# A two-block transformer kernel on one core: another order for one gate's loads, a place of the weights' ring for exponentials, 64-row products in alternation, and a later spare chunk

## The chip, the cores and the metric

The kernel runs on one core of a Trainium2 chip. The metric is the device time of one execution in microseconds (us); lower is better. Engines are named as in the profile: PE (TensorE, its weight loads apart as PEld), DVE (VectorE), ACT (ScalarE), POOL (GpSimd) and SP (SyncE, which here issues nearly all of the transfers).

## The reference

Two blocks follow each other on one sequence of 256 rows with 1024 features, all in float32. The first block has two layers, each with a mixer and a feed-forward part, and modulates both by a vector c:

```python
for i in range(2):
    mods = split(silu(c) @ w_ada[i] + b_ada[i], 6)          # sh1, sc1, g1, sh2, sc2, g2
    u = x * (1 + sc1) + sh1
    y = gla_mixer(u, ...) if i == 0 else chunk_attention(u, ...)   # 16 heads of 64
    x = layer_norm(ALPHA * x + (1 + g1) * y, ...)
    u = x * (1 + sc2) + sh2
    y = square(relu(u @ w1)) @ w2                            # 1024 -> 4096 -> 1024
    x = layer_norm(ALPHA * x + (1 + g2) * y, ...)
```

Attention is a softmax over q k' plus a bias per head. The second block is a hybrid mixer (a causal pool, and an attention of 8 heads of 64 over the best 64 keys, which an indexer with 8 heads of 64 scores) and a gated convolution network; both have dense products before and behind them.

## The kernel before, in words

**Products.** Every float32 product of the dense layers is made as three matmuls in a faster format (helper `mm3`, lines 266 to 268): the weight is split into a rounded part `hi` and a rest `lo`, the activations into `uh`/`hh` and `ul`/`hl`, and hi·uh, lo·uh and hi·ul are added up in one PSUM bank. Small products (attention scores, transposes, states) stay in float32.

**Weights.** They come in 316 chunks of 128 x 1024 floats (512 KB). `fetch` (L238) loads a chunk into `raw`, a ring of four places; ACT copies `hi` (L257) and DVE subtracts for `lo` (L262, in two halves near the ends of phases). `hi` and `lo` are rings of NB = 8 places. Some chunks are "spare": they are split into the memory of tiles that have nothing else to hold at that time (`qk0`/`v0` or `qk1`/`v1`), so that they take no place in the rings. `room()` says whether the next chunk may be loaded, and `prefetch` loads as far ahead as it allows.

**Phases.** Six phases use the chunks in order: the first mixer (chunks 16 to 36), feed-forward 1 (37 to 100), attention (101 to 132), feed-forward 2 (133 to 196), hybrid mixer (197 to 249), convolution network (250 to 315). `ENDS` holds 37, 101, 133, 197, 250, 316. The rows of the sequence are two halves, h = 0 and h = 1. A generator for each half walks through the chunks; h = 0 runs up to eight chunks ahead at a phase's start and end. A line of the program that `yield`s lets the loop go on to the next step of the one or the other half, so the order of instructions on every engine is the order in which these generators and the prefetch are called, moved a little by priorities.

**Modulation.** The w_ada product is made without PE: `ada_gen` loads 512 KB pieces into the same ring `raw` (L296) and adds them up on DVE, gates in a tile `acc` (L298), the others by rows (L300); eight pieces make one of shift, scale and gate. A gate's `acc` then becomes rows through two float32 matmuls (`gate_rows`, L325). A list `marks` holds pairs (chunk, steps): at a chunk between two marks, as many steps have been made as the line between them says, where a step is a piece or, once for every eight pieces, what closes their sum. All the loads, of weights and pieces, biases and rows, go through SP's one queue in program order.

**Attention.** `att_phase` handles the heads in two groups, g = 0 and 1, of eight. For each it makes q, k and v from chunks; while the v product runs, `core_scores` makes scores (L754), one bank of four heads (h = 0, 128 keys) or two heads (h = 1, 256 keys) at a time, adds the bias (L817, DVE), takes the maximum (L758, DVE), the exponentials with their sums (L760, ACT, one instruction for each head), and transposes them (L373, PE) into `pts` (L769, ACT). A head has 64 dimensions, so its product uses 64 of the 128 rows: the even heads of a pair lie on rows 0 to 63, the odd ones on rows 64 to 127. A bank holds heads of one parity. The hybrid mixer calls `core_scores` too; its indexer (L908) and the states of the first mixer (L727) are products of 64 rows of the same kind. `pts` lie in the tile `gnorm` for h = 0, and in `z` and `acc` for h = 1.

Of the kernel before, what the change touches and what calls it, by code (L numbers as in the profile page):

```python
# [20 lines left out]
NB = 8  # L21
# [164 lines left out]
class K:  # L186
# [450 lines left out]
    def gla_core(self, h, lr, q, k, v, box):  # L637
# [57 lines left out]
        S2 = self.states(h, 0, er, v, dec)  # L695
# [9 lines left out]
        if h == 0:  # L705
            self.S = S2
            self.S = self.states(h, 1, er, v, dec)
# [10 lines left out]
    def states(self, h, c, er, v, dec):  # L718

        nc = self.nc  # L720
        out = []
        r = slice(c * 64, c * 64 + 64)
        for j in range(2):
            p = self.pc()
            for d2 in range(2):
                d = j * 2 + d2
                nc.tensor.matmul(p[:, d2 * 256:d2 * 256 + 256], er[r, d * 128:d * 128 + 128], v[r, d * 256:d * 256 + 256], start=True, stop=True)  # L727
            S = self.sb(512, "bias", 4)
            if self.S is None:
                nc.scalar.activation(S, p, AF.Copy)  # L730
            else:
                for d2 in range(2):
                    hs = slice(d2 * 256, d2 * 256 + 256)
                    nc.vector.scalar_tensor_tensor(S[:, hs], self.S[j][:, hs], dec[:, j * 2 + d2, c:c + 1], p[:, hs], op0=ALU.mult, op1=ALU.add)
            out.append(S)
        return out
# [5 lines left out]
    def core_scores(self, h, qT, kT, pts, sums, score):  # L742
# [5 lines left out]
        last = None  # L748

        for n, hs in enumerate(self.banks(nb)):  # L750
            p = self.bank()
            for i, hd in enumerate(hs):
                r0 = (hd % 2) * 64
                nc.tensor.matmul(p[:, i * N:i * N + N], qT[r0:r0 + 64, hd // 2, :], kT[r0:r0 + 64, hd // 2, :N], start=True, stop=True)  # L754
            s = score(hs[0], nb, p)
            sv = s.rearrange("p (a n) -> p a n", n=N)
            mx = self.sb(4, "mx", 4)
            nc.vector.tensor_reduce(mx[:, :nb], sv, axis=AX.X, op=ALU.max, negate=True)  # L758
            for i in range(nb):
                nc.scalar.activation(sv[:, i, :], sv[:, i, :], AF.Exp, bias=mx[:, i:i + 1], accum_out=sums[:, hs[i]:hs[i] + 1])  # L760
            if last is not None:
                self.core_turn(last, pts[n - 1])
            last = s
            yield
        self.core_turn(last, pts[n])
# [31 lines left out]
    def halves(self, *tags):  # L797
        return [t[:, j * 512:j * 512 + 512] for t in (self.sb(1024, *g) for g in tags) for j in range(2)]

    def att_phase(self, h, after):  # L800
# [3 lines left out]
        for g in range(2):  # L804
# [66 lines left out]
    def hyb_phase(self, h, after):  # L871
# [32 lines left out]
        for hs in self.banks(nb):  # L904
            p = self.bank()
            for i, hd in enumerate(hs):
                r0 = (hd % 2) * 64
                nc.tensor.matmul(p[:, i * N:i * N + N], iqT[r0:r0 + 64, hd // 2, :], self.ikT[r0:r0 + 64, :N], start=True, stop=True)  # L908
            rl = self.cs()[:, :512]
            nc.scalar.activation(rl, p, AF.Relu, scale=0.125)  # L910
            for i, hd in enumerate(hs):
                if hd == 0:
                    nc.vector.tensor_scalar(sc, rl[:, 0:N], iw[:, 0:1], None, op0=ALU.mult)
                else:
# [478 lines left out]
```

## Time and profile before

| | |
|---|---|
| median of 3 runs | 1059.1 us (1054.99 to 1060.17) |
| the profiled execution | 1057.73 us, of which its span is 1055.9 us |
| granted TensorE clock, mean | 0.995 |
| PE busy | 1017.6 us, 96% of the span |
| DVE busy | 763.3 us, 72% |
| ACT busy | 567.6 us, 54% |
| transfers | 229 MB, 217 GB/s over the span |

The page is one execution. The shares are means over the whole span, and PE, the busiest, has about 38 us in which it is not busy; the places of these gaps can be read from the chain of waits and the timelines. A record's time on PE overlaps that of the next, so the cost of a matmul is seen in the distance between starts.

### The profile page before, as it was taken

How to read it: one execution, taken by the hardware profiler on the slowest of the kernel's cores; microseconds unless marked ns; L12 is line 12 of the kernel's file. 1: busy time of each engine (PE TensorE's matmuls, PEld its weight loads, DVE VectorE, ACT ScalarE, POOL GpSimd, SP SyncE). 2: the span in 40 equal slices, each digit the busy share in tenths (PEclk: the TensorE clock that was granted, in tenths of full speed). 3: DMA queues.
4: the chain of work that ended last, by engine and by line, in shares of the span. 5: the costliest groups of instructions: out<-in, count | busy, mean ns of one | idle time of the engine just before them, and what ended most of it. 6: DMA issues, size and time to landing. Idle time of an engine off the chain costs nothing.

```text
span 1055.9 us, 15168 instructions
## 1 busy us (share of the span) xinstructions
PE 1017.6 (96%) x5628; PEld 850.0 (80%) x5628; DVE 763.3 (72%) x1186; ACT 567.6 (54%) x869; POOL 33.8 (3%) x77
## 2 busy tenths in 40 slices
PE   6999999999998999999999999999999999999997
PEld 4777777898986758677889988777878788999996
DVE  6878898777677886749656644898445678877764
ACT  4664466545455454536655553576454378555543
POOL 0000200000000000000000000000000001000000
PEclk9999999999999999999999999999999999999999
DMA  9888868888885787825877654344346455655521
GB/s 341 331 298 301 309 201 282 306 304 298 284 297 179 218 295 247 286 92 184 287 229 249 227 166 145 120 145 149 106 164 213 162 179 182 217 185 192 183 80 40
DMA packets 69478, 228.98 MB, mean 217 GB/s; under 512 B 7430, under 2 KB 12806, under 8 KB 69404
## 3 DMA queue, kind: packets, MB, share of 16 engines
q1 hardware_dynamic: 69404, 228.01, 64.2%
q8 instruction: 44, 0.72, 0.3%
q14 instruction: 30, 0.25, 0.1%
HBM read 226.93 MB, written 1.05 MB: 216 GB/s over the span
## 4 chain that ended last, share of the span: by engine, by line
PE 63%; DVE 9%; DMA 7%; ACT 3%; issue 3%; POOL 1%; POOLq 0%; DVEq 0%; ACTq 0%; SPq 0%
PE ps L268 12%; PE ps L266 12%; PE ps L267 12%; PE y L266 8%; PE y L268 8%; PE y L267 7%; DMA raw<-in_w_dram 6%; DVE lo L262 2%; PE y L780 1%; PE pc L373 1%; ACT hi L257 1%; DMA raw<-in_ada_dram 1%; PE y L373 1%; PE y L754 1%; DVE x L393 1%
## 5 line engine op out<-in xcount | busy, mean ns | idle before, releaser
L262 DVE TENSOR_TENSOR lo<-raw,hi 128x1024 fp32r<-128x1024 f32 (+3 forms) x290 | 306.5, 1068 | 132.8 <-ACT hi L257 129.4
L257 ACT ACTIVATE hi<-raw 128x1024 fp32r<-128x1024 f32 (+2 forms) x250 | 262.4, 1054 | 252.1 <-PE y L268 66.9
L266 PE MATMUL ps<-hi,uh 128*128 128x512 f32 (+3 forms) x408 | 160.4, 394 | 2.3 <-ACT uh L365 0.9
L267 PE MATMUL ps<-lo,uh 128*128 128x512 f32 (+3 forms) x408 | 158.2, 388 | 1.2 <-DVE lo L1260 1.1
L266 PE MATMUL y<-hi,hh 128*128 128x512 f32 x378 | 152.9, 404 | 5.3 <-ACT hh L274 5.2
L268 PE MATMUL ps<-hi,ul 128*128 128x512 f32 (+3 forms) x408 | 157.5, 386 | 0.2 <-DVE ul L366 0.2
L267 PE MATMUL ps<-ul,hi 128*128 128x256 f32 x536 | 151.4, 282 | 0.0
L268 PE MATMUL ps<-uh,lo 128*128 128x256 f32 x536 | 151.1, 282 | 0.0
L266 PE MATMUL ps<-uh,hi 128*128 128x256 f32 x536 | 151.0, 282 | 0.0
L268 PE MATMUL y<-hi,hl 128*128 128x512 f32 x378 | 149.8, 398 | 0.4 <-DVE hl L275 0.4
L267 PE MATMUL y<-lo,hh 128*128 128x512 f32 x378 | 150.2, 397 | 0.0
L266 PEld LDWEIGHTS ps<-uh,hi 128*128 128x128 f32 x536 | 100.9, 188 | 2.3
L267 PEld LDWEIGHTS ps<-ul,hi 128*128 128x128 f32 x536 | 100.6, 188 | 2.3
L268 PEld LDWEIGHTS ps<-uh,lo 128*128 128x128 f32 x536 | 101.3, 189 | 0.0
L266 PEld LDWEIGHTS ps<-hi,uh 128*128 128x128 f32 x408 | 77.5, 190 | 19.3 <-ACT uh L365 1.5
L267 PEld LDWEIGHTS ps<-lo,uh 128*128 128x128 f32 x408 | 77.5, 190 | 16.8 <-DVE lo L1260 3.0
L268 PEld LDWEIGHTS ps<-hi,ul 128*128 128x128 f32 x408 | 77.4, 190 | 15.8 <-issue 0.9
L266 PEld LDWEIGHTS y<-hi,hh 128*128 128x128 f32 x378 | 71.5, 189 | 21.4 <-ACT hh L274 6.6
L268 PEld LDWEIGHTS y<-hi,hl 128*128 128x128 f32 x378 | 71.3, 189 | 18.2 <-DVE hl L275 1.2
L267 PEld LDWEIGHTS y<-lo,hh 128*128 128x128 f32 x378 | 71.4, 189 | 14.8 <-issue 0.7
L262 DVE TENSOR_TENSOR v<-raw,qk 128x1024 fp32r<-128x1024 f32 (+1 forms) x49 | 52.0, 1069 | 26.7 <-ACT qk L257 26.1
L257 ACT ACTIVATE qk<-raw 128x1024 fp32r<-128x1024 f32 x42 | 44.5, 1060 | 49.7 <-DMA raw<-in_w_dram 28.7
(290 smaller groups left out, 1500.0 us busy)
## 6 DMA issues: line engine op xcount, KB each, us to landing
raw<-in_w_dram SPq DMA_DIRECT2D x302, 512.0 KB, 4.3
raw<-in_ada_dram SPq DMA_DIRECT2D x80, 512.0 KB, 4.6
br<-in_rows_dram SPq DMA_DIRECT2D x12, 256.0 KB, 5.4
bias<-in_relb_dram SPq DMA_DIRECT2D x12, 256.0 KB, 6.2
lng<-in_rows_dram SPq DMA_DIRECT2D x5, 512.0 KB, 4.8
raw<-in_w_dram SPq DMA_DIRECT2D x8, 256.0 KB, 6.7
lnb<-in_rows_dram SPq DMA_DIRECT2D x4, 512.0 KB, 6.1
z<-in_ada_dram SPq DMA_DIRECT2D x3, 512.0 KB, 7.4
```

What stands on the lines that cost most here:

```text
L257: self.nc.scalar.activation(hi, raw, AF.Copy)
L262: self.nc.vector.tensor_sub(lo[:, sl], raw[:, sl], hi[:, sl].bitcast(F32))
L266: mm(out, xh, wh, start=start, stop=False)
L267: mm(out, xh, wl, start=False, stop=False)
L268: mm(out, xl, wh, start=False, stop=stop)
L373: self.nc.tensor.transpose(p[:, k * 128:k * 128 + 128], src[:, k * 128:k * 128 + 128], self.ident)
L393: nc.vector.tensor_mul(x[:, sl], x[:, sl], self.lng[:, sl])
L754: nc.tensor.matmul(p[:, i * N:i * N + N], qT[r0:r0 + 64, hd // 2, :], kT[r0:r0 + 64, hd // 2, :N], start=True, stop=True)
L780: nc.tensor.matmul(o[:, hd * 64:hd * 64 + 64], pT[:, (i * nkb + kb) * 128:(i * nkb + kb) * 128 + 128], v[:, kb, hd * 64:hd * 64 + 64], sta ...
```

## The change

1. `marks`: while feed-forward 1 runs, 24 pieces are loaded (before: 32), and the burst of eight pieces behind chunk 116 is gone; the 24 pieces after those come between chunk 108 and the end of the attention. The first gate of the second layer is so added up in `acc` during the attention, and its two matmuls (L325) go from the first group of heads to the second.
2. Since `acc` is taken then, `pts` of h = 1 lie in `z` and in one place of the ring `hi`; `room()` leaves that place out while the attention's chunks are loaded.
3. Scores, indexer and states: two banks of different parity are filled in alternation, head by head, and everything behind them (bias, maximum, exponentials, transposes) is written two banks at a time. The states of both 64-row chunks of h = 0 are made together.
4. The first spare chunk of feed-forward 2 is 138 and no longer 134. Both use `qk0`/`v0`, which chunk 129 held before them.

```diff
-                        (ENDS[2] + 1, ENDS[3] + 1, (0, 1)), (ENDS[4] - 8, ENDS[5], (0, 1))):
+                        (ENDS[2] + 5, ENDS[3] + 1, (0, 1)), (ENDS[4] - 8, ENDS[5], (0, 1))):
...
+                for c, p in enumerate(ps):
+                    r = slice(c * 64, c * 64 + 64)
+                    nc.tensor.matmul(p[:, d2 * 256:d2 * 256 + 256], er[r, d * 128:d * 128 + 128], v[r, d * 256:d * 256 + 256], start=True, stop=True)
...
+        groups = self.banks(nb)
+        last = []
+
+        for n in range(0, len(groups), 2):
+            two = groups[n:n + 2]
+            ps = [self.bank() for _ in two]
+            for hs in zip(*two):
+                for p, hd in zip(ps, hs):
+                    i = two[hd % 2].index(hd)
+                    r0 = (hd % 2) * 64
+                    nc.tensor.matmul(p[:, i * N:i * N + N], qT[r0:r0 + 64, hd // 2, :], kT[r0:r0 + 64, hd // 2, :N], start=True, stop=True)
...
+            for m, s in enumerate(last):
+                self.core_turn(s, pts[n - 2 + m])
+            last = new
             yield
-        self.core_turn(last, pts[n])
+            yield
+        for m, s in enumerate(last):
+            self.core_turn(s, pts[n + m])
...
-                    pts = self.halves(("gnorm", 1)) if h == 0 else self.halves(("z", 1), ("acc", 1))
+                    pts = self.halves(("gnorm", 1)) if h == 0 else self.halves(("z", 1)) + self.halves(("hi", NB, F32R))
...
-        marks = [(15, 0), (F0, F1), (M0, 27), (ENDS[0] + 8, 27), (ENDS[1] - M1, 62), (ENDS[1] + 7, 62), (ENDS[1] + 8, 63 + FINK), (ENDS[2] - AE, 81), (ENDS[2] + 12, 81), (ENDS[3] - 20, 90)]
+        marks = [(15, 0), (F0, F1), (M0, 27), (ENDS[0] + 8, 27), (ENDS[1] - M1, 54), (ENDS[1] + 4, 54), (ENDS[2] - AE, 81), (ENDS[2] + 12, 81), (ENDS[3] - 20, 90)]
...
-            return sum(i not in SPARE for i in live) < NB
+            return sum(i not in SPARE for i in live) < NB - (ENDS[1] + 4 <= self.loaded < ENDS[2])
```

In the rows below, the first number is that of the instruction on its engine and the last number of a name only counts tiles; it differs between the two kernels.

**SP's queue at the start of the attention.** `raw<-in_w_dram` is a weight chunk, `raw<-in_ada_dram` a piece. Before, the burst stands behind chunk 116 (`raw_3429`):

```order
217 L238 DMA raw_3397<-in_w_dram 128x1024
218 L238 DMA raw_3409<-in_w_dram 128x1024
219 L238 DMA raw_3429<-in_w_dram 128x1024
220 L296 DMA raw_3436<-in_ada_dram 128x1024
221 L296 DMA raw_3439<-in_ada_dram 128x1024
222 L296 DMA raw_3442<-in_ada_dram 128x1024
223 L296 DMA raw_3445<-in_ada_dram 128x1024
224 L296 DMA raw_3448<-in_ada_dram 128x1024
225 L296 DMA raw_3451<-in_ada_dram 128x1024
226 L296 DMA raw_3454<-in_ada_dram 128x1024
227 L296 DMA raw_3457<-in_ada_dram 128x1024
```

In the changed kernel three pieces stand between chunks 108 (`raw_3209`) and 109 (`raw_3316`), and then, from chunk 116 (`raw_3496`) on, one behind each chunk; chunk 118 is `raw_3586`:

```order
199 L238 DMA raw_3209<-in_w_dram 128x1024
200 L296 DMA raw_3266<-in_ada_dram 128x1024
201 L296 DMA raw_3275<-in_ada_dram 128x1024
202 L296 DMA raw_3284<-in_ada_dram 128x1024
203 L238 DMA raw_3316<-in_w_dram 128x1024
...
217 L238 DMA raw_3496<-in_w_dram 128x1024
218 L296 DMA raw_3502<-in_ada_dram 128x1024
219 L238 DMA raw_3517<-in_w_dram 128x1024
220 L296 DMA raw_3523<-in_ada_dram 128x1024
221 L826 DMA bias_3556<-in_relb_dram 128x2x256
222 L826 DMA bias_3565<-in_relb_dram 128x2x256
223 L238 DMA raw_3586<-in_w_dram 128x1024
```

What moved: the burst of eight behind chunk 116 is gone, and pieces alternate with chunks in its place; four transfers before chunk 118 stands chunk 116, whose place in `raw` it takes.

**PE in the first group of heads.** Before, the products of one bank (`y`) stand together, and the gate's matmuls (L325) split one bank's four heads:

```order
1678 L754 MATMUL y_3478<-qk_668_3243,ep_677_3285 128x128 x2
1679 L373 MATMUL pc_3423<-const_70,t_707_3421 128x128 x4
1680 L325 MATMUL pc_3461<-acc_2646,ones_65 128x512
1681 L325 MATMUL pc_3464<-acc_2646,ones_65 128x512
1682 L754 MATMUL y_3478<-qk_668_3243,ep_677_3285 128x128 x2
...
1689 L754 MATMUL y_3506<-qk_668_3243,ep_692_3368 128x256 x2
...
1705 L754 MATMUL y_3558<-qk_668_3243,ep_692_3368 128x256
1706 L373 MATMUL y_3546<-const_70,cs_3486 128x128
1707 L754 MATMUL y_3558<-qk_668_3243,ep_692_3368 128x256
```

In the changed kernel two banks take turns (L761 is the scores' line there), here those of h = 1 with 256 keys:

```order
1723 L268 MATMUL ps_3421<-hi_3351,ul_73 128x512
1724 L761 MATMUL y_3550<-qk_659_3215,ep_684_3347 128x256
1725 L761 MATMUL y_3551<-qk_659_3215,ep_684_3347 128x256
1726 L761 MATMUL y_3550<-qk_659_3215,ep_684_3347 128x256
1727 L761 MATMUL y_3551<-qk_659_3215,ep_684_3347 128x256
1728 L266 MATMUL ps_3421<-hi_3366,uh_72 128x512
...
1742 L373 MATMUL y_3608<-const_70,cs_3559 128x128 x4
1743 L373 MATMUL y_3614<-const_70,cs_3568 128x128 x4
1744 L792 MATMUL y_3638<-v_660_3216,gnorm_3420 128x64 x4
```

What moved: products of one bank no longer follow each other, and the transposes of both banks (L373) stand behind twelve dense matmuls and eight other transposes, which are rows 1728 to 1741.

**ACT and DVE at the same place, changed kernel.** On ACT the exponentials of these two banks (L769, `cs_3559` and `cs_3568`) stand around the splitting of chunk 118 (L257 with `raw_3586`) and the copies of the transposes (L781):

```order
264 L781 ACTIVATE z_3463<-y_3574 128x512
265 L781 ACTIVATE z_3463<-y_3580 128x512
266 L257 ACTIVATE hi_3588<-raw_3586 128x1024
267 L769 ACTIVATE cs_3559,sums_3462<-cs_3559,mx_3561 128x256 x2
268 L781 ACTIVATE hi_3464<-y_3608 128x512
269 L769 ACTIVATE cs_3568,sums_3462<-cs_3568,mx_3570 128x256 x2
```

On DVE the `lo` of chunk 116 (`raw_3496`) stands behind the bias of these scores (L829):

```order
363 L298 SCALAR_TENSOR_TENSOR acc_3262<-raw_3523,cact_83,acc_3262 128x1024
364 L829 TENSOR_TENSOR cs_3559<-y_3550,bias_3556 128x512
365 L262 TENSOR_TENSOR lo_3499<-raw_3496,hi_3498 128x1024
366 L262 TENSOR_TENSOR lo_3520<-raw_3517,hi_3519 128x1024
367 L767 TENSOR_REDUCE mx_3561<-cs_3559 128x2
```

Before, two instructions of L760, one for each of the two banks of a pair, stood with the splitting of a chunk and one copy of transposes between them; now both banks' exponentials stand behind the splitting of a chunk which has to be loaded into the place that `lo_3499` frees.

**ACT at the end of the attention.** Before, `qk_921` is chunk 134, split into the memory of chunk 129:

```order
307 L257 ACTIVATE hi_4343<-raw_4341 128x1024
308 L257 ACTIVATE hi_4350<-raw_4348 128x1024
309 L257 ACTIVATE hi_4357<-raw_4355 128x1024
...
314 L365 ACTIVATE uh_72<-t_910_4254 128x512
315 L257 ACTIVATE qk_921_4336<-raw_4334 128x1024
316 L257 ACTIVATE hi_4364<-raw_4362 128x1024
317 L365 ACTIVATE uh_72<-t_911_4261 128x512
```

In the changed kernel chunk 138 (`qk_933`) takes that memory:

```order
306 L257 ACTIVATE hi_4209<-raw_4207 128x1024
307 L257 ACTIVATE hi_4287<-raw_4285 128x1024
308 L257 ACTIVATE hi_4304<-raw_4302 128x1024
309 L257 ACTIVATE hi_4321<-raw_4319 128x1024
...
315 L257 ACTIVATE hi_4351<-raw_4349 128x1024
316 L257 ACTIVATE qk_933_4364<-raw_4362 128x1024
317 L365 ACTIVATE uh_72<-t_911_4261 128x512
```

What moved: chunk 134 is split with its neighbours, and the splitting that has to wait for the old user of `qk0`/`v0` is that of a chunk needed four chunks later.

## Rows read from the trace of the kernel before

**Rows 1.** Chain of waits on PE: us in total, times, longest us

```profile
PE y L266 <- ACT hh L274: 5.4, 3, 4.4
PE y L373 <- ACT cs L760: 2.9, 4, 1.3
PE ps L267 <- DVE v L262: 2.3, 1, 2.3
PE pc L373 <- DVE t L869: 1.8, 1, 1.8
```

**Rows 2.** Windows (us: busy us by engine, PE clock, DMA share, GB/s)

```profile
321.00:325.80 4.80, 0.40 (x3) 0.07 (x1) 2.59 (x5) 2.80 (x4) 0.00 (x0) 0.99 0.94 344
326.00:329.00 3.00, 3.00 (x8) 2.28 (x9) 0.71 (x2) 0.00 (x0) 0.00 (x0) 0.50 0.68 183
364.00:442.00 78.00, 73.36 (x360) 54.47 (x358) 57.65 (x82) 40.53 (x88) 1.60 (x7) 1.00 0.82 280
482.00:485.20 3.20, 0.89 (x5) 0.41 (x3) 3.20 (x8) 0.00 (x0) 0.00 (x0) 1.00 0.00 0
486.00:489.00 3.00, 3.00 (x9) 2.36 (x9) 2.56 (x6) 0.81 (x1) 0.84 (x1) 0.53 0.60 190
```

**Rows 3.** Timeline of ACT at the end of feed-forward 1

```profile
322.81 1.06 ACT L257 ACTIVATE hi<-raw 128x1024 fp32r<-128x1024 f32 x1 [1.94 <-DMA raw<-in_w_dram]
```

**Rows 4.** Timeline of PE at the same place

```profile
325.73 0.79 PE L266 MATMUL y<-hi,hh 128*128 128x512 f32 x1 [4.40 <-ACT hh L274]
...
329.25 0.39 PE L268 MATMUL y<-hi,hl 128*128 128x512 f32 x1
329.48 0.40 PE L266 MATMUL y<-hi,hh 128*128 128x512 f32 x1
```

**Rows 5.** Transfers, 171 to 313 us: count, KB each, us to landing

```profile
raw<-in_w_dram SPq DMA_DIRECT2D x47, 512.0 KB, 4.8
raw<-in_ada_dram SPq DMA_DIRECT2D x32, 512.0 KB, 4.8
```

**Rows 6.** Timeline of PE in the first group of heads

```profile
371.32 2.04 PE L325 MATMUL pc<-acc,ones 128*128 128x512 f32 x4
373.29 0.71 PE L754 MATMUL y<-qk,ep 64*128 64x128 f32 x4
373.93 0.50 PE L266 MATMUL ps<-hi,uh 128*128 128x512 f32 x1
...
375.53 1.13 PE L754 MATMUL y<-qk,ep 64*128 64x256 f32 x4
376.58 0.50 PE L266 MATMUL ps<-hi,uh 128*128 128x512 f32 x1
```

**Rows 7.** Timeline of PE in the hybrid mixer

```profile
727.32 1.17 PE L754 MATMUL y<-qk,ep 64*128 64x256 f32 x12
728.66 0.33 PE L373 MATMUL y<-const,cs 128*128 128x128 f32 x1 [0.17 <-ACT cs L760]
```

**Rows 8.** Timeline of ACT between exponentials, first group of heads

```profile
388.79 1.06 ACT L257 ACTIVATE hi<-raw 128x1024 fp32r<-128x1024 f32 x1 [2.23 <-DMA raw<-in_w_dram]
389.75 0.39 ACT L760 ACTIVATE cs<-cs,mx 128x128 f32<-128x128 f32 x1
...
391.29 0.49 ACT L760 ACTIVATE cs<-cs,mx 128x256 f32<-128x256 f32 x1
```

**Rows 9.** Groups of DVE by shape, 364 to 447 us

```profile
L262 DVE TENSOR_TENSOR lo<-raw,hi 128x1024 fp32r<-128x1024 f32 x17 | 20.7, 1221 | 8.2 <-ACT hi L257 8.2
L300 DVE SCALAR_TENSOR_TENSOR raw<-raw,crow 128x1024 f32<-128x1024 f32 x15 | 18.3, 1220 | 7.1 <-DMA raw<-in_ada_dram 7.0
```

**Rows 10.** Chain of waits on DVE, 364 to 442 us

```profile
DVE raw L300 <- DMA raw<-in_ada_dram: 7.0, 5, 3.1
```

**Rows 11.** Timelines of ACT and DVE at the end of the attention

```profile
478.41 1.07 ACT L257 ACTIVATE qk<-raw 128x1024 fp32r<-128x1024 f32 x1
...
484.43 0.67 DVE L262 TENSOR_TENSOR v<-raw,qk 128x512 fp32r<-128x512 f32 x1
```

More of the change, by code (lines that the diff above doesn't have):

```diff
@@ L694, in gla_core @@
         yield
-        S2 = self.states(h, 0, er, v, dec)
+        S2, *S3 = self.states(er, v, dec, 2 - h)
         o = self.py()
@@ L705, in gla_core @@
         if h == 0:
-            self.S = S2
-            self.S = self.states(h, 1, er, v, dec)
+            self.S = S3[0]
         yield
@@ L716, in gla_core, with states @@
         box["r"] = r
-    def states(self, h, c, er, v, dec):
+    def states(self, er, v, dec, n):
         nc = self.nc
-        out = []
-        r = slice(c * 64, c * 64 + 64)
+        out = [[], []]
         for j in range(2):
-            p = self.pc()
+            ps = [self.pc() for _ in range(n)]
             for d2 in range(2):
                 d = j * 2 + d2
[L727 to L736, printed above, removed]
+                for c, p in enumerate(ps):
+                    r = slice(c * 64, c * 64 + 64)
+                    nc.tensor.matmul(p[:, d2 * 256:d2 * 256 + 256], er[r, d * 128:d * 128 + 128], v[r, d * 256:d * 256 + 256], start=True, stop=True)
+            for c, p in enumerate(ps):
+                S = self.sb(512, "bias", 4)
+                before = out[0][j] if c else self.S and self.S[j]
+                if before is None:
+                    nc.scalar.activation(S, p, AF.Copy)
+                else:
+                    for d2 in range(2):
+                        hs = slice(d2 * 256, d2 * 256 + 256)
+                        nc.vector.scalar_tensor_tensor(S[:, hs], before[:, hs], dec[:, j * 2 + d2, c:c + 1], p[:, hs], op0=ALU.mult, op1=ALU.add)
+                out[c].append(S)
+        return out[:n]
     @staticmethod
@@ L747, in core_scores @@
         nb = 512 // N
[L748 to L763, printed above, removed]
+        groups = self.banks(nb)
[8 more added lines that the diff above has]
+                    nc.tensor.matmul(p[:, i * N:i * N + N], qT[r0:r0 + 64, hd // 2, :], kT[r0:r0 + 64, hd // 2, :N], start=True, stop=True)
+            new = []
+            for hs, p in zip(two, ps):
+                s = score(hs[0], nb, p)
+                sv = s.rearrange("p (a n) -> p a n", n=N)
+                mx = self.sb(4, "mx", 4)
+                nc.vector.tensor_reduce(mx[:, :nb], sv, axis=AX.X, op=ALU.max, negate=True)
+                for i in range(nb):
+                    nc.scalar.activation(sv[:, i, :], sv[:, i, :], AF.Exp, bias=mx[:, i:i + 1], accum_out=sums[:, hs[i]:hs[i] + 1])
+                new.append(s)
+            for m, s in enumerate(last):
+                self.core_turn(s, pts[n - 2 + m])
+            last = new
             yield
-        self.core_turn(last, pts[n])
+            yield
+        for m, s in enumerate(last):
+            self.core_turn(s, pts[n + m])
     def core_turn(self, s, pT):
@@ L797, in halves @@
     def halves(self, *tags):
-        return [t[:, j * 512:j * 512 + 512] for t in (self.sb(1024, *g) for g in tags) for j in range(2)]
+        return [t[:, j * 512:j * 512 + 512].bitcast(F32) for t in (self.sb(1024, *g) for g in tags) for j in range(2)]
     def att_phase(self, h, after):
```

27 lines of the change are left out of this document (15 added, 12 removed).

## Prediction

> **What bounds the kernel now.** PE is busy nearly everywhere, so I first read what it waits for, in the chain of waits on PE [rows 1], and then looked for the place of each long wait in the windows [rows 2] and timelines. Three places touch this change.
>
> The largest is the end of feed-forward 1. From 321.0 to 325.8 us PE is busy for 0.40 us, while the transfers are at 0.94 of their share and 344 GB/s [rows 2]. PE stands 4.40 us for an activation half, `hh`, until 325.73 [rows 4]; ACT, which makes it, had stood 1.94 us for a weight chunk and splits that at 322.81 [rows 3], ahead of the last column's work in its order. So a late weight of the attention, in ACT's order ahead of the last column of feed-forward 1, holds PE. What makes it late are 47 chunks and 32 pieces of 512 KB between 171 and 313 us [rows 5]: 79 x 0.524 MB in 142 us is 292 GB/s, little under what the transfers reach when nothing else limits them. The granted clock is 0.50 from 326 to 329, the lower of its two levels, after this pause [rows 2].
>
> The second is the turn from attention to feed-forward 2: PE waits 2.3 us for `v`, L262 [rows 1], the `lo` of spare chunk 134, which DVE makes in two halves from 484.43 on, although ACT had made the other part at 478.41 [rows 11]. DVE is full meanwhile: 3.20 of 3.20 us between 482.0 and 485.2 [rows 2]. Behind it the clock stands at 0.53 for 3.0 us.
>
> The third is the attention. Between 364 and 442 us PE is busy 73.36 of 78 us [rows 2], so it is idle for 4.6 us there; 2.9 us of waits are for exponentials (L760) [rows 1].
>
> **Part 1, pieces moved.** Feed-forward 1 loses 8 of its 79 transfers: 71 x 0.524 MB in the 142 us are 262 GB/s, a tenth less than now and well under the 344. The lag at its end, 4.40 + the 1.94 us of ACT and what led to them, was built up by these loads, and eight of them at 292 GB/s are 14.4 us of transfer. The chunk that blocks ACT then comes over 10 us earlier, so I take all of the wait away, and the clock's loss with it: 3.00 us at 0.50 is 1.5 us. Together 4.4 + 1.5 = **5.9 us**. Its lower bound is about 4 (a rest of the wait stays, for the `hi` place or ACT's own queue), its upper 6.5 (the shorter waits on `hh` make 1.0 more in [rows 1]).
>
> What is paid for it: eight more sums on DVE in the attention, of 1.22 us as the other pieces there [rows 9], 9.8 us. DVE was busy 57.65 of 78 us there [rows 2], so it has room, but its order is fixed: a sum that waits for its piece holds everything behind it. Such waits took 7.0 us in 5 cases, the longest 3.1 [rows 10]. Weights can bear the extra transfers, since 0.82 of the DMA share is in use [rows 2] and the burst of eight goes. The gate's two matmuls (2.04 us with a piece of the transposes beside them, [rows 6]) leave the first group and enter the second: nothing in the sum.
>
> **Part 2, a place of the `hi` ring.** It takes one of eight places from the prefetch during the attention. The weights there are ahead by more than one chunk's time, and that is what hides it; without this cover ACT would wait as in [rows 8], 2.23 us at a time. I count 0, with -2.2 to 0 as bounds.
>
> **Part 3, alternation.** A bank's run of two products of 128 columns (x4 records, two for each float32 product) takes from 373.29 to 373.93, 0.64 us, and one of two with 256 columns from 375.53 to 376.58, 1.05 us [rows 6]. What two row groups give when they follow each other is already in the trace once: in the hybrid mixer a bank of odd heads happens to stand directly behind one of even heads, and twelve records (four products of 128 columns, two of 256) take 1.17 us [rows 7], where single runs would cost 2 x 0.64 + 1.05 = 2.33. So alternation halves the time: records of the two groups run beside each other.
>
> The attention has 16 products of 128 and 16 of 256 columns: 8 x 0.64 + 8 x 1.05 = 13.5 us now, 6.8 then, a gain of **6.8 us** on PE. Its lower bound is nothing (if PE merely waits in the time that it has won), its upper about 8, since the single products of the first group, which transposes now separate, also become runs. In the hybrid mixer six products of 256 columns are left, 3.15 us, so 1.6 us at most. There PE went on 0.17 us behind an exponential already [rows 7], so I take a third, **0.5 us**. The indexer I count at nothing: PE stands 1.8 us for DVE (L869) behind it [rows 1], and a faster score only lengthens that wait; the cover gone, it would be worth 0.8. The states are 0 to 0.5, and I take 0: the second half still waits for the first.
>
> The Trainium skill says of such packing, in TensorEngine Tiling (Array Packing), Performance Considerations, that it speeds up TensorE but not the emptying of PSUM, so that this may become the bottleneck. By that rule the 6.8 us would bring nothing where a core waits for its softmax; the trace agrees so far that exponentials already make PE wait 2.9 us. It is the third rival below.
>
> What hangs on the scores is not made faster: a bias of 128x512 on DVE, some 0.67 us like the other work of this shape [rows 11], four exponentials of 128 columns from 389.75 to 391.29, 1.54 us [rows 8]. And the order gets one new hazard. In the first group the third pair's exponentials stand on ACT behind the splitting of chunk 118. That chunk's place in `raw` is freed by the `lo` of chunk 116, which stands on DVE behind the bias of the same scores. From the scores' end: bias 0.67, `lo` 1.22 [rows 9], landing 4.8 [rows 5], splitting 1.06 and two exponentials of 0.5 each [rows 8], 8.8 us in a row. PE has twelve dense matmuls of 0.23 [rows 4] and eight transposes, each at most 0.16 as a record of 128 columns in [rows 6], until it needs them, 4.1 us. The wait could so be 4.7 us, or nothing if the chunk's place comes free earlier than its order says. Before, ACT stood 2.23 us for a chunk ahead of exponentials in the same way [rows 8], and PE's longest wait for them was 1.3 [rows 1]. I take 3.5 for the new one, nearer to the sum of the rows, and 0.5 for a piece that stands before a maximum in the second group (bound 3.1, [rows 10]). The attention's net is 6.8 - 4.0 = **2.8 us** (from -1.5 to 8).
>
> **Part 4, spare chunk.** Chunk 134 is then split in the ring, early, and the 2.3 us go, with 3.00 x 0.47 = 1.4 us of the clock: 3.7 at most. But DVE stays full with the layer norm there, and chunks 136 and 137 follow on it at about 486 and 488 us; PE would run into their `lo` next. I take **2 us** (0 to 3.7).
>
> **The sum**, against the profiled execution of 1057.73 us: 5.9 + 2.8 + 0.5 + 2.0 = 11.2, so 1046.5. That execution is 1.4 us below the median of the runs; on the median it is 1059.1 - 11.2 = 1047.9, so **1048 us**. With its terms at their own bounds the likeliest case lies between 1041 and 1054.
>
> **Rivals.** First, all of PE's savings arrive: the chain above hides, since the place in `raw` comes free in time. 5.9 + 6.8 + 1.6 + 3.7 = 18 us, and up to 20 with the upper bounds: 1039 to 1041. For it speaks that DVE is a quarter idle in the attention; against it, that the order of ACT and DVE is fixed.
>
> Second, the attention takes all its own gain back and the turn to feed-forward 2 keeps its wait under another chunk's name. 5.9 stay, from which waits beyond the savings (the 4.7 us of the chain, 1.5 of a lower clock behind it, a piece or two of 3.1 us, against 6.8) take 1 to 4: 1054 to 1058. For it speaks that every instruction behind a late piece waits, and DVE stays full at the turn.
>
> Third, the softmax is the bound of the core: no gain from alternation at all, and only parts 1 and 4 count, 5.9 + 2.0: 1051. It is inside the likeliest case's range, and the place where the rule of the skill would put it.
>
> On the other side: the pieces on DVE stand ahead of the bias and maximum of the scores, where they wait for their transfers as L300 did 5 times in the 78 us [rows 10], now for 24 pieces in place of 16. If eight more such waits of up to 3.1 us each reach PE with the chain of chunk 118, 25 + 4.7 us stand against 18 us of gains. It decides from 18 us of new waits on PE; at all of them it is 1059 + 12 = 1071, at two thirds 1061 to 1065. Against it: before, DVE stood 7.0 us for pieces [rows 10], and PE was idle for only 4.6 us there for all causes together.
>
> That the pieces moved don't relieve the end of feed-forward 1 (ACT's order blocks it whatever the load) would leave 5.3 of the 11.2: 1054, part of the second rival's band.
>
> **Chances.** The likeliest case with the third rival 0.58; all savings 0.18; the second rival 0.18, of which two thirds are within 0.5% (5.3 us, about what a measurement of this kernel can tell from none); the slower side 0.06. So faster 0.80, same 0.14, slower 0.06. Eight in ten lie between the first rival's 1038 and the second's 1058.
>
> **What would show it.** Right: no wait on `hh` of over 1 us at the end of feed-forward 1 and a clock at its upper level there; score runs of eight records in about half of their time; a wait of PE for `cs` (exponentials) of 2 to 5 us in the first group behind the third pair, with ACT standing for a transfer at chunk 118; a smaller wait at the turn, for chunks 136 or 137. Wrong: waits for pieces on DVE that show up on PE; alternating records as long as before; a new wait for `hi` in the attention, since a place is gone; chunk 109, now behind three pieces, late for the second half of feed-forward 1.

## The result, and the profile after

The changed kernel takes 1048.9 us in the median of 8 runs (1045.0 to 1053.23), the kernel before 1057.05 us in 8 runs beside it. The ratio is 0.9918, with a 95% interval of 0.9891 to 0.9945: some 8.7 us less by the ratio, 8.15 between the medians. The forecast was 1048 us. The profiled execution of after is one of its longer ones (span 1050.1 us, 5.8 less than that of before), so the sum has to be read stage by stage.

I took, in every trace, the start of the first of the three matmuls of each dense product, numbered them (1608 in each), and compared the time between the same products. Each column is the change of one stage in us, against the profile of before, from the first of these products on; the rows behind the first are the experiments below, 1 to 10 in order.

```
                  start,   feed-   end of  begin  att.   att.   turn   feed-  hybrid hybrid conv.
                  mixer 1  fwd 1   ff 1    att.   grp 0  grp 1  to ff2 fwd 2  pt. 1  pt. 2
after              1.73    0.60   -6.21   -0.02  -1.72   4.06  -2.80  -0.45  -2.04   1.15  -0.15
no alternation     0.06   -0.30   -6.21   -0.02  -3.77   5.39  -3.40  -0.13  -0.41  -0.01  -0.12
alternation alone -1.29    0.89   -4.15   -0.02  -0.68  -1.81  -0.10  -0.37  -1.81   1.13  -0.02
spare 138 alone    0.75   -0.45   -0.59   -0.01   4.20  -0.31  -3.28  -0.27  -0.41  -0.01  -0.11
spare 134 back    -0.04    0.28   -6.21   -0.01  -1.58   1.84  -0.27   0.13  -1.83   1.14  -0.15
banks in turn     -0.52    0.73   -6.21   -0.03  -1.95   3.54  -3.49  -0.25  -2.06   0.62  -0.14
v first            1.28    0.18   -6.21   -0.02  -4.76  -2.66  -3.42  -0.60  -2.06   1.15  -0.10
v and bias first   0.55   -0.03   -6.21   -0.02  -3.88  -1.42  -3.77  -0.55  -2.04   1.15  -0.14
short sums         1.63   -0.11   -6.21    0.31  -6.02  -0.98  -3.42  -0.24  -2.06   1.14   0.23
before, v first    0.07    0.14   -0.95   -0.02   2.02   0.19  -1.33  -0.23  -0.01   0.00  -0.17
no altern., v fst -1.61    0.22   -6.21   -0.03  -3.13  -1.84  -2.34  -0.26  -0.41  -0.01  -0.15
```

The first column moves also where nothing in that stage was edited (-1.61 without alternation and v first, 0.75 with the spare chunk alone): that is the start's own scatter. So do others: the first group of heads is 4.20 and 2.02 us longer in two rows without an edit there (runs 3 and 9), whose granted clock is low there (0.53 from 390 to 401 us, 0.51 from 390 to 397); the turn is 1.33 shorter in run 9, and the end of feed-forward 1 is 0.59 to 4.15 shorter in the three runs that leave the pieces where they were (2, 3, 9). A single entry is weak; the rows agree where they share an edit.

**End of feed-forward 1.** In windows of after (time, busy us of PE, PEld, DVE, ACT, POOL, then PE clock, DMA share, GB/s) the stall of [rows 2, 4] is gone and the clock stays at its upper level; the second line is where a new pause was, the third answers to the attention's window in [rows 2]:

```profile
317.00:326.00 9.00, 9.00 (x40) 7.26 (x39) 2.87 (x5) 1.76 (x4) 0.00 (x0) 1.00 0.54 188
446.00:453.00 7.00, 7.00 (x26) 5.93 (x25) 4.35 (x9) 0.27 (x1) 0.00 (x0) 0.51 0.76 248
364.00:442.00 78.00, 71.06 (x377) 54.36 (x375) 61.81 (x84) 44.58 (x100) 2.73 (x10) 0.98 0.88 286
```

PE is busy for 9.00 of 9.00 us and the transfers, at 0.94 before, are at 0.54. But between 364 and 442 us PE is idle for 6.9 us in place of 4.6, and DVE is busy 61.81 in place of 57.65.

**What PE waits for now**, in the chain of waits on PE of after (us in total, times, longest), against [rows 1]:

```profile
PE y L792 <- DVE v L846: 2.9, 1, 2.9
...
PE y L373 <- DVE cs L829: 2.2, 1, 2.2
PE pc L373 <- DVE t L881: 2.1, 3, 1.6
PE pc L373 <- DVE t L851: 1.6, 3, 0.9
PE y L373 <- ACT gnorm L781: 1.5, 1, 1.5
PE y L373 <- ACT cs L769: 1.5, 2, 1.2
```

Neither `hh` nor the split of a spare chunk (L262) is in the list any more. New are `v` (L846), which the attention's output product needs, and two waits of transposes (L373) for a bank in PSUM that DVE's bias addition (L829) or ACT's copy (L781) has to empty.

**First group of heads.** In the timelines of after, first PE and then DVE:

```profile
377.40 1.14 PE L761 MATMUL y<-qk,ep 64*128 64x256 f32 x8
...
381.35 1.09 PE L373 MATMUL y<-const,cs 128*128 128x128 f32 x4 [2.15 <-DVE cs L829]
...
386.69 0.93 PE L373 MATMUL y<-const,cs 128*128 128x128 f32 x4 [0.35 <-ACT cs L769]
388.79 0.93 PE L373 MATMUL y<-const,cs 128*128 128x128 f32 x4 [1.17 <-ACT cs L769]
```

```profile
376.72 1.28 DVE L298 SCALAR_TENSOR_TENSOR acc<-raw,cact,acc 128x1024 f32<-128x1024 f32 x1 [1.62 <-DMA raw<-in_ada_dram]
...
379.32 1.28 DVE L298 SCALAR_TENSOR_TENSOR acc<-raw,cact,acc 128x1024 f32<-128x1024 f32 x1 [0.61 <-DMA raw<-in_ada_dram]
380.52 0.68 DVE L829 TENSOR_TENSOR cs<-y,bias 128x512 f32<-128x512 f32 x1
```

The scores of 377.40 are done within about a microsecond; their first bias addition comes at 380.52. Of the two pieces ahead of it the first ends before the scores do; the second, with 0.61 us of waiting for its transfer, holds DVE from 378.7 to 380.5. PE's transposes wait 2.15 us for the bank that the addition empties. With the 0.35 and 1.17 for exponentials this is 3.7 us. Behind the 2.15 the clock is at its lower level as well, which the window shows:

```profile
382.00:385.00 3.00, 3.00 (x12) 2.49 (x11) 3.00 (x5) 1.46 (x4) 0.00 (x0) 0.54 1.04 285
```

That is 3.00 x 0.46 = 1.4 us more in this execution.

**Second group of heads.** The same for the second group, PE and DVE:

```profile
435.58 1.14 PE L761 MATMUL y<-qk,ep 64*128 64x256 f32 x8
438.26 1.14 PE L373 MATMUL y<-const,cs 128*128 128x128 f32 x8 [1.55 <-ACT gnorm L781]
...
445.14 1.10 PE L792 MATMUL y<-v,gnorm 128*128 128x64 f32 x8 [2.93 <-DVE v L846]
446.05 0.67 PE L266 MATMUL ps<-hi,hh 128*128 128x512 f32 x1
446.52 0.63 PE L267 MATMUL ps<-lo,hh 128*128 128x512 f32 x1
446.95 0.63 PE L268 MATMUL ps<-hi,hl 128*128 128x512 f32 x1
```

```profile
442.04 1.23 DVE L300 SCALAR_TENSOR_TENSOR raw<-raw,crow 128x1024 f32<-128x1024 f32 x1 [0.54 <-DMA raw<-in_ada_dram]
443.19 0.08 DVE L300 DVE_READ_ACCUMULATOR raw<-raw,crow 128x1 f32 x1
443.19 1.29 DVE L262 TENSOR_TENSOR lo<-raw,hi 128x512 fp32r<-128x512 f32 x2
444.40 0.68 DVE L846 TENSOR_TENSOR v<-ps,br 128x512 f32<-128x512 f32 x1
```

PE has made v's product by 442.2, but DVE takes a piece (with 0.54 us of waiting) and a `lo` first and adds v's bias at 444.40. PE stands 2.93 us, and the clock is at 0.51 from 446 to 453, which is 7.00 x 0.49 = 3.4 us more: dense matmuls that start every 0.43 us. The wait comes again in every run with the pieces moved, summed in full and v in its old place, 2.9 to 3.6 us (runs 1, 4 and 5). The lower clock behind it doesn't: in run 4, the same code here, PE waits as long at the same instruction, and the clock stays at its upper level (timeline and window of run 4):

```profile
443.98 1.10 PE L792 MATMUL y<-v,gnorm 128*128 128x64 f32 x8 [2.94 <-DVE v L846]
```

```profile
444.00:454.00 10.00, 9.92 (x57) 8.33 (x58) 9.19 (x20) 2.64 (x4) 0.00 (x0) 1.00 0.93 314
```

The second group is 1.84 us longer there, where it is 4.06 in after.

### The profile page after: what moved, and what is told of

Read it like the earlier page. It is cut to its first block, busy times and chain, and to the rows that moved or that the text cites. A ratio compares the mean times of both kernels' runs of the same rounds, so it can differ in the third digit from the quotient of the medians.

```text
span 1050.1 us, 15144 instructions
## 1 busy us (share of the span) xinstructions
PE 1010.6 (96%) x5628; PEld 846.7 (81%) x5628; DVE 760.3 (72%) x1186; ACT 567.1 (54%) x869; POOL 34.7 (3%) x77
## 4 chain that ended last, share of the span: by engine, by line
PE 61%; DVE 11%; DMA 5%; issue 4%; ACT 3%; POOL 1%; SPq 0%; POOLq 0%; DVEq 0%; ACTq 0%
PE ps L266 11%; PE ps L268 11%; PE ps L267 11%; PE y L266 8%; PE y L268 8%; PE y L267 8%; DMA raw<-in_w_dram 4%; DVE lo L262 3%; PE y L792 1%; DMA raw<-in_ada_dram 1%; ACT hi L257 1%; PE pc L373 1%; DVE x L393 1%; DVE ul L366 1%; DVE x L394 1%
## 5 line engine op out<-in xcount | busy, mean ns | idle before, releaser
L257 ACT ACTIVATE hi<-raw 128x1024 fp32r<-128x1024 f32 (+2 forms) x251 | 263.6, 1054 | 265.7 <-DMA raw<-in_w_dram 93.5
L262 DVE TENSOR_TENSOR lo<-raw,hi 128x1024 fp32r<-128x1024 f32 (+3 forms) x293 | 307.7, 1062 | 127.6 <-ACT hi L257 125.6
L300 DVE SCALAR_TENSOR_TENSOR raw<-raw,crow 128x1024 f32<-128x1024 f32 x48 | 58.3, 1220 | 21.0 <-DMA raw<-in_ada_dram 21.0
L257 ACT ACTIVATE qk<-raw 128x1024 fp32r<-128x1024 f32 x41 | 43.4, 1059 | 38.6 <-DMA raw<-in_w_dram 19.9
```

Of the source, the lines that this page charges most:

```text
L257: self.nc.scalar.activation(hi, raw, AF.Copy)
L262: self.nc.vector.tensor_sub(lo[:, sl], raw[:, sl], hi[:, sl].bitcast(F32))
L300: nc.vector.scalar_tensor_tensor(raw, raw, 1.0, self.crow, op0=ALU.mult, op1=ALU.mult, accum_out=t[:, k:k + 1])
```

## The experiments

All ratios are to the kernel before, over runs of it taken beside those of each experiment, with their 95% interval.

**1. Everything but the alternation.** The kernel before with the edits of `marks`, `pts`, `room` and the spare chunk; `core_scores`, the indexer and the states are as before.

```diff
-                    pts = self.halves(("gnorm", 1)) if h == 0 else self.halves(("z", 1), ("acc", 1))
+                    pts = self.halves(("gnorm", 1)) if h == 0 else self.halves(("z", 1)) + self.halves(("hi", NB, F32R))
...
-            return sum(i not in SPARE for i in live) < NB
+            return sum(i not in SPARE for i in live) < NB - (ENDS[1] + 4 <= self.loaded < ENDS[2])
```

> The kernel before with the pieces moved, the place of the hi ring and spare chunk 138, but the scores one bank at a time. Theory A (the pieces on DVE cause the attention's new waits, and alternation gives its 6.8 us of PE): the gains of 6.2 at the end of feed-forward 1 and 3.7 at the turn stay, the attention loses about 3.6 + 6.8 = 10 us, so no change against before, ratio 0.998 to 1.003. Theory B (writing two banks at a time causes the new waits, the pieces cost little): the attention is within 1 us of before, so about 9 us faster, ratio 0.991.

Measured: 1048.85 us, ratio 0.9935 (0.9915 to 0.9954). Neither theory's number, and the time of after (1048.9 us): on top of the other edits the alternation brings nothing that these times show. The table says why it is neither. The gate's two matmuls (2.04 us, [rows 6]) change group in all runs with the pieces moved, so both groups have to be read together: the first is 3.77 us shorter, the second 5.39 longer, 1.6 in all, without any pair of banks. The second group's loss is there without alternation (theory A), but the attention's is far smaller than that theory had it, and nearer to theory B's 1 us. PE waits for v as in after:

```profile
PE y L780 <- DVE v L834: 3.3, 1, 3.3
```

**2. Alternation alone.** The changed kernel with the four other edits undone.

```diff
-                    pts = self.halves(("gnorm", 1)) if h == 0 else self.halves(("z", 1)) + self.halves(("hi", NB, F32R))
+                    pts = self.halves(("gnorm", 1)) if h == 0 else self.halves(("z", 1), ("acc", 1))
...
-                        (ENDS[2] + 5, ENDS[3] + 1, (0, 1)), (ENDS[4] - 8, ENDS[5], (0, 1))):
+                        (ENDS[2] + 1, ENDS[3] + 1, (0, 1)), (ENDS[4] - 8, ENDS[5], (0, 1))):
```

> The kernel before with the alternating products alone: pieces, ring and spare chunk as before. Theory A: attention 5 to 7 us shorter, hybrid mixer 1.5, the stall of 4.4 us at the end of feed-forward 1 and the wait of 2.3 at the turn as before: 7 to 8 us faster, ratio 0.993. Theory B: attention 1 to 3 us longer than before or equal, hybrid mixer 1.5 shorter: ratio 0.998 to 1.002.

Measured: 1051.45 us, ratio 0.995 (0.9929 to 0.9971), between the theories. The attention is 2.5 us shorter (0.68 + 1.81) and the hybrid mixer 0.7, though PE's time for the attention's scores falls from 13.7 to 8.1 us (from the first record of a run to the next instruction, waits left out, added up over the runs). Waits for exponentials don't take the difference, since they are as long as before (2.8 us; 2.9 in [rows 1]). The clock takes most of it: it is at its lower level twice in the attention (windows), some 3 us each time at half speed, and nowhere in the attention of before:

```profile
PE y L373 <- ACT cs L769: 2.8, 2, 2.4
PE y L266 <- ACT hh L274: 1.8, 2, 1.5
```

```profile
382.50:385.50 3.00, 3.00 (x10) 1.89 (x10) 1.46 (x4) 2.73 (x10) 0.40 (x2) 0.50 1.05 400
433.60:436.60 3.00, 3.00 (x8) 2.03 (x8) 1.38 (x4) 3.00 (x12) 0.20 (x1) 0.50 1.02 388
```

The stall for `hh` was shorter in this profile than in that of before (1.8 for 5.4 us), though nothing here acts on it: without the change it differs between executions.

**3. The spare chunk alone.**

```diff
-                        (ENDS[2] + 1, ENDS[3] + 1, (0, 1)), (ENDS[4] - 8, ENDS[5], (0, 1))):
+                        (ENDS[2] + 5, ENDS[3] + 1, (0, 1)), (ENDS[4] - 8, ENDS[5], (0, 1))):
```

> The kernel before with spare chunk 138 in place of 134, nothing else. If that is the whole cause of the wait at the turn, the 2.3 us for v and the lower clock behind it go and nothing takes their place: 3 to 4 us faster, ratio 0.9965, all of it between the last products of the attention and the first of feed-forward 2. Rival, as the prediction's sum had it: chunks 136 and 137, split late on DVE, stop PE next, so that 2 us remain, ratio 0.998.

Measured: 1054.03 us, ratio 0.9973 (0.9946 to 1.0). The time doesn't tell the two apart, and the turn's column of -3.28 does so weakly, since it is -1.33 in run 9 without this edit. PE's waits do: between 476 and 500 us it waits 0.5 us for the norm's `x` and 0.2 for `hh`, and for no chunk. In windows of the turn, which comes some 3 us later here than in [rows 2], PE is busy throughout at the upper clock, while DVE is as full as before:

```profile
482.00:485.20 3.20, 3.20 (x16) 2.56 (x15) 3.20 (x7) 2.86 (x4) 0.00 (x0) 1.00 0.79 282
486.00:489.00 3.00, 3.00 (x15) 2.40 (x14) 3.00 (x8) 1.06 (x1) 0.00 (x0) 1.00 0.00 0
```

Nothing takes the place of chunk 134's wait.

**4. The spare chunk back.** The changed kernel with chunk 134 spare again (the diff of run 3 the other way round).

> The changed kernel with chunk 134 spare again in place of 138. If the spare chunk is the cause of the wait at the turn, the wait of 2.3 us for v and the lower clock behind it come back: 3 to 4 us slower than the changed kernel, ratio to before about 0.995. Rival (the other parts moved DVE's work there so that the wait goes in any case): no difference from the changed kernel, 0.992.

Measured: 1051.47 us, ratio 0.9965 (0.9946 to 0.9984). The time is 2.6 us above that of after. The wait is back, in two parts, and the turn's column is -0.27 where after has -2.80:

```profile
PE ps L267 <- DVE v L262: 1.6, 2, 1.3
```

**5. Banks in turn.** The changed kernel, with the products of a pair written bank by bank.

```diff
-            for hs in zip(*two):
-                for p, hd in zip(ps, hs):
-                    i = two[hd % 2].index(hd)
+            for p, hs in zip(ps, two):
+                for i, hd in enumerate(hs):
```

> The changed kernel, with the products of a pair of banks written one bank behind the other instead of head by head in turn; all that follows is as in the changed kernel. If PE's time for the products is what counts there, 24 products more or less in series cost 5 to 8 us against the changed kernel, ratio to before 0.997 to 0.999. If the softmax behind the scores is the bound, the difference is 0 to 2 us, 0.992 to 0.994, and PE's waits for cs shrink by what the products grow.

Measured: 1049.16 us, ratio 0.9926 (0.99 to 0.9952), the same as after. But it didn't tell the two theories apart, since the products took hardly longer. A pair of banks of 256 columns, one written behind the other, in the timeline of PE:

```profile
434.42 1.14 PE L760 MATMUL y<-qk,ep 64*128 64x256 f32 x8
435.49 0.33 PE L373 MATMUL y<-const,cs 128*128 128x128 f32 x1
```

Eight records from 434.42 to 435.49, as in after with heads in turn, and as four of one row group in [rows 6]. All runs of scores in the attention take 8.4 us here, 7.25 in after, 13.7 before. What gives the gain is that two banks of different parity stand together, not that heads alternate.

**6. v first.** The changed kernel with a priority for one instruction, so that DVE has v's addition ahead of the pieces.

```diff
-                    nc.vector.tensor_add(v[:, h, :], self.res, br)
+                    with self.tc.high_priority(offset=HPE):
+                        nc.vector.tensor_add(v[:, h, :], self.res, br)
```

> The changed kernel with a priority for the addition that makes v from its product, so that DVE's order has it ahead of the pieces. Theory A (in the second group PE waits 2.9 us for v because a piece and its transfer stand ahead of it on DVE, and the clock falls behind that wait): that wait is under 1 us and the clock stays at its upper level; 4 to 6 us faster than the changed kernel, ratio to before 0.986 to 0.988. Rival (v is late because the softmax work ahead of it is late, not because of the piece): the wait stays at 2 us or more, ratio 0.991 to 0.992.

Measured: **1040.35 us, ratio 0.9843** (0.9801 to 0.9886), 8.5 us below after: theory A, and more than its 4 to 6 us. PE's waits have no entry for this v, and the clock holds through the place of the former pause (windows):

```profile
PE y L373 <- DVE cs L829: 2.1, 1, 2.1
PE y L373 <- ACT gnorm L781: 1.6, 1, 1.6
```

```profile
440.00:455.00 15.00, 15.00 (x82) 12.63 (x82) 10.89 (x23) 3.69 (x5) 0.00 (x0) 1.00 0.82 279
```

The second group is 6.7 us shorter than in after (-2.66 for 4.06), about the 2.93 and the 3.4 of the clock in that profile; against run 4, without the clock's part, it is 4.5. The first group is 3.0 us shorter as well (-4.76 for -1.72): the waits for exponentials there fall from 1.5 to 0.3 us, and no lower clock follows the wait for the bank. Why the exponentials come earlier is not shown.

**7. v and bias first.** As run 6, with the same priority for the bias additions to the scores.

```diff
-                nc.vector.tensor_add(s.rearrange("p (a n) -> p a n", n=N), p.rearrange("p (a n) -> p a n", n=N), bias[:, :, ::-1])
+                with self.tc.high_priority(offset=HPE):
+                    nc.vector.tensor_add(s.rearrange("p (a n) -> p a n", n=N), p.rearrange("p (a n) -> p a n", n=N), bias[:, :, ::-1])
```

> As the run with v first, and the same priority for the additions of the bias to the scores. Theory A, for the first group (there PE waited 2.15 us for a bank that the bias addition empties, while DVE stood for a piece): that wait goes too, 2 to 4 us more than v first alone, ratio to before 0.983 to 0.986. Rival (the softmax of two banks is simply longer than what PE has beside it): the waits move to the exponentials and the ratio is that of v first.

Measured: 1040.73 us, ratio 0.9841 (0.9805 to 0.9877), no more than v first: the rival's number, though the waits move to the exponentials only in part. The wait for the bank falls from 2.1 to 0.3, and others grow, for DVE's sums ahead of the q and k transposes above all:

```profile
PE pc L373 <- DVE t L853: 2.9, 3, 1.2
PE y L373 <- ACT cs L769: 1.1, 1, 1.1
```

**8. Short sums.** The changed kernel with 8 of 1024 columns summed of the 24 pieces in the attention; all are loaded.

```diff
+                m = 8 if 6 <= idx <= 8 else 1024
                 if gate:
-                    nc.vector.scalar_tensor_tensor(acc, raw, self.cact[:, k:k + 1], acc, op0=ALU.mult, op1=ALU.add)
+                    nc.vector.scalar_tensor_tensor(acc[:, :m], raw[:, :m], self.cact[:, k:k + 1], acc[:, :m], op0=ALU.mult, op1=ALU.add)
```

(The same for the other kind of sum.)

> The changed kernel, where the 24 pieces that come during the attention are loaded as before but only the first 8 of their 1024 columns are summed, so that DVE's part of a piece takes some 0.1 us in place of 1.22; a piece still waits for its transfer. The sums left out change the modulation of the second layer. If DVE's time for the pieces is what the attention lost, about 8 us come back there (first and second group 2 to 4 us shorter than in the kernel before): ratio to before 0.984. If the waits of the pieces for their transfers are what it lost, at most 2 us: ratio 0.990 to 0.992.

Measured: 1040.82 us, ratio 0.9839 (0.9803 to 0.9875). The pieces still wait for their transfers on DVE, longer than in after (9.4 us between 364 and 447; 4.6 in after), and yet the loss is gone (the two groups together are 7.0 us shorter than before):

```profile
DVE acc L299 <- DMA raw<-in_ada_dram: 4.8, 3, 2.5
DVE raw L301 <- DMA raw<-in_ada_dram: 4.6, 3, 2.9
```

So it is the 1.22 us that DVE works for each piece, ahead of what PE needs, and not the pieces' transfers. The shorter sums also moved a few instructions of DVE's order, so the share of order and of work is not separated here.

**9. The kernel before with v first.** The edit of run 6 on the kernel before.

> The kernel before with the priority for v's addition alone. Theory (the priority repairs what the moved pieces broke): PE has no wait of over 0.5 us for v in the attention of before, so there is nothing to win, ratio 0.998 to 1.002. Rival (the order of v and the pieces costs the kernel before as well, and the gain of some 8 us is that of another change): 4 us or more faster, ratio 0.996 or less.

Measured: 1056.98 us, ratio 1.0003 (0.9977 to 1.003). Nothing to win there: PE has no wait for v in the attention of this run, so the late v came with the pieces.

**10. No alternation, with v first.** The edit of run 6 on run 1.

> The run without alternation, with the priority for v. It tells what the two-bank products are worth once the wait for v is gone. If PE's 6.5 us for the scores then arrive, this run is 5 to 7 us slower than the changed kernel with v first (ratio to before 0.984), so 0.989 to 0.991, with the attention 4 to 6 us longer and the hybrid mixer 1 us. If the softmax still takes most of them back, 0.986 to 0.988.

Measured: 1042.47 us, ratio 0.9872 (0.9841 to 0.9903), 2 to 3 us above run 6, with overlapping intervals, so that the time by itself doesn't tell the two apart. The attention is 2.5 us longer than in run 6 (-4.97 for -7.42), the hybrid mixer 0.5. The clock is at its upper level through the attention of both, so these stages can be compared; windows over it, first of run 6, then of this run:

```profile
350.00:455.00 105.00, 99.81 (x534) 78.51 (x534) 84.62 (x122) 55.52 (x115) 2.80 (x10) 1.00 0.88 293
355.00:462.00 107.00, 105.46 (x535) 81.20 (x535) 84.61 (x127) 55.68 (x115) 3.35 (x11) 1.00 0.84 284
```

PE is idle for 5.2 us in run 6 and for 1.5 here, where it has hardly a wait:

```profile
PE pc L373 <- DVE t L840: 1.2, 2, 1.0
...
PE y L373 <- ACT cs L760: 0.5, 1, 0.5
```

So of 6.5 us that PE saves on the attention's scores some 2.5 arrive, and run 6 shows where most of the rest is: 2.1 and 1.6 us of waits for a bank, which this run doesn't have.

## Why the prediction was right, and where it was not

The time was right, 1048.9 for 1048 us, and in part by luck. The stages behind the first column add to -7.6 us in the profiles, and the medians differ by 8.15; the prediction had -11.2, on a median of before that was 2 us higher. So a gain that was some 3 us too large was taken off a start that was 2 us too high. Within the gain the attention was 5 us too good, and the turn, the mixer and feed-forward 1 together 1.5 too poor.

**End of feed-forward 1, -5.9 us: right for this profile of before.** It is -6.2, in every run with the pieces moved, and no `hh` wait is left there. The three other runs that leave the pieces where they were have less to win, since their stage is 0.59 to 4.15 us shorter than that of the profiled before: against the mean of the four the edit is worth 4.8. The ring's place went with the pieces in every run, so the two are not told apart. The price, eight more sums on DVE, entered the sum with no more than the 0.5 that is quoted below, and there the loss comes from.

**Attention, -2.8 us: the gain did not arrive.** The two columns add to +2.3 in the profile of after and to +0.3 in that of run 4, which has the same code there. The products' part was right: 6.8 us were forecast, and PE's time for the scores fell from 13.7 to 7.25, by 6.5. (Its 2.33 us for single runs should be 2.1, since the eight records of a whole bank of four heads take 1.09 us in before, from 378.18, and not 2 x 0.64; heads that stood alone cost more, so that 13.5 still comes near 13.7. By its own terms the upper bound of part 1 is 6.9 and not 6.5.) In the first group 3.5 us of new wait were set against it, and 3.7 came (with 1.3 for exponentials there before) and 1.4 of clock behind it, but not by the chain that was described: ACT did not stand for chunk 118, DVE had a piece ahead of a bias addition, and PE stood for the bank. That the number fits is luck. The step that failed is "0.5 for a piece that stands before a maximum in the second group" (bound 3.1). There a piece stood before v's addition, and PE waited 2.93 us; in the profiled execution another 3.4 us of clock followed, 6.3 in all, in run 4 none. The prediction had charged the clock at both junctions of before, but at none of the waits in its sum (its second rival had 1.5). Runs 1, 6, 8 and 9 show that the pieces' work on DVE ahead of v is the cause of the wait: it is there without alternation (3.3), it goes when v goes ahead, it shrinks to 1.1 when the sums are short, and moving v wins nothing where the pieces are not.

**The ring's place, 0: as forecast on PE.** No wait of PE for a `hi` appeared in the attention. But the weights came later than the prediction took it: ACT's waits for them between 355 and 447 us, first before and then after, are nearly three times as long; which of the edits does this is not separated.

```profile
ACT hi L257 <- DMA raw<-in_w_dram: 7.4, 6, 2.2
ACT hi L257 <- DMA raw<-in_w_dram: 21.2, 10, 4.7
```

**Turn to feed-forward 2, -2.0 us: too small.** It is -2.8 to -3.8 in all but one of the runs with chunk 138 spare (-2.34 in run 10), the whole wait of 2.3 and, by the most of these, the clock behind it, 3.7 together by [rows 2]. The clock's part is not there in every execution: run 9 waits 2.3 us at the same place, keeps its clock, and has -1.33 without the edit. The expected next wait, for chunks 136 and 137, did not come although DVE is as full as before: PE has no wait for them in run 3 or in after.

**Hybrid mixer, -0.5 us: -0.9.** The table's two parts meet at a product around which the scores changed places, so only their sum says something: -0.9 in after, -0.7 with the alternation alone, and -0.4 without it in the runs with chunk 138 spare (1, 3 and 10), which the prediction did not have. Between products 1041 and 1071 of the count, where the scores stand, PE's time for them falls from 5.4 to 3.8 us, which is the whole 1.6 of the bound. What takes it back are the transposes, now eight in a row (3.4 us for 2.7), and waits of 0.9 us in place of 0.2, the longest for a bank that ACT's copy (L781) empties:

```profile
730.70 1.14 PE L373 MATMUL y<-const,cs 128*128 128x128 f32 x8 [0.46 <-ACT acc L781]
```

**The rivals.** The softmax as the bound is partly true: as the kernel stands, run 1 has the time of after and so none of the savings shows; with the late v out of the way, 2.5 of 6.5 us arrive, and waits for a bank hold much of the rest (run 7, which shortens one of them, was no faster). The rule of the Trainium skill that the prediction weighed (TensorEngine Tiling (Array Packing), Performance Considerations: packing speeds up TensorE but not the emptying of PSUM) agrees with the 2.1 and 1.6 us of run 6. The slower side did not come: its sign, pieces on DVE that show up on PE, was there, but in two places (2.15 and 2.93 us) and not in eight.

## What to carry to other kernels

Work moved out of a place where transfers are the bound has to be charged on the engine that it joins by its place in that engine's fixed order, not by that engine's idle share: here 1.2 us of DVE work for a piece, and a `lo` behind it, ahead of one addition cost PE a wait of 2.9 us, and one priority won some 8 us where a whole planning change had won 8.7. A forecast that counts a wait of 2 us and more on PE should carry the lower clock behind it as a range, here from nothing to 3.4 us. A profile of one execution has its own share of that, so a stage's price should be read from more than one. And after packing two products beside each other, look for the wait for an empty PSUM bank.

## What the hardware showed that was not expected

Products of the two row groups run beside each other even when they are written one group behind the other: in run 5 eight records, four of each group, take from 434.42 to 435.49, 1.07 us, as long as four of one group did before (375.53 to 376.58 in [rows 6]). [rows 7] had shown it before the change, which run 5's expectation overlooked: eight records of 128 columns and four of 256, two banks written one behind the other, take 1.17 us, and three of the eight and two of the four have started within the first 0.4 us (matmuls of L754 in the window 727.3 to 727.7 of before):

```profile
L754 PE MATMUL y<-qk,ep x5: 272/373/480, 727.3 to 727.7; 64*128 64x128 f32 x3, 64*128 64x256 f32 x2
```

In after, the pause of 2.93 us was followed by some 7 us at a granted clock of 0.51, the lower level of 1.2 GHz, and that of 2.15 us by 3 us at 0.54. With v first, a pause of nearly the same length at the same place (2.08 us, for the same bank) was followed by none: dense matmuls behind it start every 0.23 us. Two pairs of executions show the same for the same code: the 2.93 us of after stand beside the 2.94 of run 4, which no lower clock followed, and the 2.31 us at the turn of before, with 3 us at 0.53 behind them [rows 2], beside the 2.31 of run 9, whose clock stayed (window):

```profile
486.20:489.20 3.00, 2.99 (x12) 2.10 (x13) 2.56 (x8) 0.81 (x1) 0.92 (x1) 1.00 0.33 52
```

So what a pause costs behind itself can't be told from its length alone.
